# A new order of the 32 experts in a mixture-of-experts stage: small and large ones by turns

## The chip, the core and the metric

The kernel runs on one core of one Trainium2 chip. The metric is the device time of the core in microseconds (us). The kernel before takes 4002.02 us, the median of three runs (3997.02 to 4007.37). The core's engines are named as in the profile: PE (matmuls; PEld its weight loads), DVE (vector work), ACT (activations and copies), POOL (here gathers and scatters through indirect DMA), SP (issues the DMAs of the weights).

## What is computed

The reference is two transformer-like blocks. The change touches the last stage of the second, a mixture of 32 experts over 512 tokens with four experts for each token. Cut to what matters:

```python
logits = (h @ w_router).astype(jnp.float32) + b_router.astype(jnp.float32)
top_val, top_idx = lax.top_k(logits, TOP_K)          # TOP_K = 4 of 32 experts
gates = jax.nn.softmax(top_val, axis=-1)
# for every expert e, on its tokens x:
#   u = x @ w1[e] + b1[e]              # 1024 -> 2048, (gate, linear) pairs
#   a = min(silu-like(u_gate), limit) * (clip(u_lin) + 1)
#   y = a @ w2[e] + b2[e]              # 1024 -> 1024
# the output of a token is the sum of its four y, weighted by gates
```

The last lines are a summary in words of the block function of the reference.

## The kernel before, in words

Before the stage the kernel sorts the experts by the number of tokens that they got (`in_order`). A **rank** is a place in that sorted list; rank 0 is always expert 0, whose first weights are loaded early. `CAPS` fixes how many rows are computed for each rank: 128 for rank 0, 192 for ranks 1 and 2, 128 for ranks 3 to 9, 96 for ranks 10 to 15 and 64 for ranks 16 to 31. "Small" means 64 rows below, "large" 96 and more. Tokens beyond the capacity go to a loop behind the stage, which runs no round in the profiled execution.

The table `ORDER` (L38) lists the ranks in the sequence in which they are computed. In turn i of the loop (L2129) the kernel does `up` of the expert at place i (L1931; `up_half`, L1945, for 192 rows and for the last place), and beside it `down` of the expert at place i-1 (L1964; `down_two`, L1978). An expert draws 12 chunks of weights of 1 MB: eight for `up`, four for `down`. SP loads them into eight buffers (`stage`, L1680). PE multiplies in a fast form that needs a chunk split into two parts: ACT writes the high part `mh` (L1833), DVE the low part `ml` (L1834, 128x2048), three and two buffers of these. `into` (L1872) then issues the matmuls of a chunk for `mh` and `ml` (L1882), and the bias matmuls behind the first chunk (L1886). Experts of 64 rows are "packed": high and low parts of the tokens share one matmul, and on chunks 1 and 4 of `up` and 1 and 2 of `down` the weights are taken unsplit (L1877). So a small expert needs fewer splits and fewer matmuls than a large one.

Beside these a turn holds the preparation of later experts. `Rows` of the next expert transposes its gathered tokens (PE, `pcol`, L1865), and ACT and DVE write them in parts (`ch`, `cl`, L1867 to L1870). `place` of the expert two places on (L2096) calls `gather` (L1897): DVE builds `oh` (L1904), PE computes the token numbers `pi` by four short matmuls (L1907), DVE turns them into an index in a chain of small instructions on `ix` (L1909 to L1914), and POOL fetches the tokens by an indirect DMA (L1916) into `XT`. The results of `up` pass `gated` (L1922, ACT and DVE; packed ones first `whole`, L1888, with an ACT copy and a DVE addition `cl`), those of `down` pass `weighed` (L1956), whose DVE instruction L1959 scales `py` and whose POOL instruction L1961 adds the rows to the output.

Each engine runs its instructions in one fixed order, which a scheduler sets when the program is built; it takes what is ready by its own estimate, so the position of `pi`, of the transposes and of `ml` within a turn depends on which experts are neighbours. The two calls that issue the preparation stand in the loop as

```python
if end and k == (ATC if nparts == 4 else 1) and i < 31:
    xs = [Rows(b[2], "x") for b in got[i + 1][0]]
if end and k == (2 if nparts == 4 else 1) and i < 30:
    got[i + 2] = place(ORDER[i + 2])
```

Of the kernel before, what the change touches and what calls it, by code (L numbers as in the profile page):

```python
# [34 lines left out]

PLAIN = ((1, 4), (1, 2))

ORDER = [0, 16, 17, 18, 1, 19, 20, 21, 2] + list(range(3, 16)) + list(range(22, 32))  # L38

CAPS = [128] + [192] * 2 + [128] * 7 + [96] * 6 + [64] * 16  # L40
OVB = 20
# [87 lines left out]
def tile_two_blocks(ctx: ExitStack, tc: tile.TileContext, I: dict, out: bass.AP, dump=None, stop=None):  # L129
# [1966 lines left out]
    def place(r):  # L2096

        lb = wk.tile([64, 128], F32R, name="lb", tag="lb", bufs=4)
        nc.vector.tensor_copy(lb, (SELP[:, r:r + 1] if r else sel[0:64, 0:1]).to_broadcast([64, 128]))
        pos = lambda t: POS[:, 32 * t + r:32 * t + r + 1]  # L2100
        col = (lambda t: COL[:, t, r, :]) if r else (lambda t: COL0[:, t, 0, :])
        return [gather(pos, col, a, min(128, CAPS[r] - a)) for a in range(0, CAPS[r], 128)], lb
# [23 lines left out]
    xs = [Rows(b[2], "x") for b in got[0][0]]  # L2126
    got[1] = place(ORDER[1])
    before, acts = None, []
    for i in range(33):  # L2129
        steps = [None]  # L2130
        if i < 32:
            blocks, lb = got.pop(i)
            r = ORDER[i]
            e = 0 if r == 0 else nc.sync.value_load(OI[0:1, r:r + 1], min_val=0, max_val=31)
# [18 lines left out]
        for step in steps:  # L2153
# [5 lines left out]
            for k in range(nparts):  # L2159
# [9 lines left out]
                if end and k == (2 if nparts == 4 else 1) and i < 30:  # L2169
                    got[i + 2] = place(ORDER[i + 2])  # L2170
        for _ in todo or ():
# [49 lines left out]
```

## Time and profile before

| | |
|---|---|
| median of three runs | 4002.02 us |
| the profiled execution: time | 3993.1 us |
| the profiled execution: span of the trace | 3991.2 us |
| PE busy | 3767.5 us, 94% of the span |
| DVE busy | 2726.4 us, 68% |
| ACT busy | 1693.6 us, 42% |
| POOL busy | 331.3 us, 8% |
| mean granted clock of PE | 0.961 |
| the expert turns, rank 0 to the end | 2748.6 to 3991 us |

All durations come from one execution, the profiled one. The trace gives each instruction's start and length, the idle time of its engine just ahead of it and what released it. A turn is counted here from the first bias matmul of one `up` (line L1886 with `pu`) to that of the next.

### The profile page before, as it was taken

How to read it: one execution, taken by the hardware profiler on the slowest of the kernel's cores; microseconds unless marked ns; L12 is line 12 of the kernel's file. 1: busy time of each engine (PE TensorE's matmuls, PEld its weight loads, DVE VectorE, ACT ScalarE, POOL GpSimd, SP SyncE). 2: the span in 40 equal slices, each digit the busy share in tenths (PEclk: the TensorE clock that was granted, in tenths of full speed). 3: DMA queues.
4: the chain of work that ended last, by engine and by line, in shares of the span. 5: the costliest groups of instructions: out<-in, count | busy, mean ns of one | idle time of the engine just before them, and what ended most of it. 6: DMA issues, size and time to landing. Idle time of an engine off the chain costs nothing. (4 is left out here: it accounts for less than half of the span.)

```text
span 3991.2 us, 68996 instructions
## 1 busy us (share of the span) xinstructions
PE 3767.5 (94%) x27579; PEld 2829.1 (71%) x27579; DVE 2726.4 (68%) x5439; ACT 1693.6 (42%) x2528; POOL 331.3 (8%) x349
## 2 busy tenths in 40 slices
PE   6998999999999998999999998996999999999997
PEld 4787777888888787776887886674555777664443
DVE  4779875843334778876644535648877899987776
ACT  3234442321212334452222334444655676665555
POOL 0001110000000000110000000001101122223011
PEclk8999999999999998999999997997999999999999
DMA  6122423332422321124544520035979899998996
GB/s 208 45 79 72 120 70 92 125 122 79 127 85 85 103 71 25 38 56 124 169 140 135 123 67 32 1 118 210 373 272 352 314 362 360 370 354 330 375 369 240
DMA packets 353911, 677.75 MB, mean 170 GB/s; under 512 B 118759, under 2 KB 230194, under 8 KB 323474
## 3 DMA queue, kind: packets, MB, share of 16 engines
q1 hardware_dynamic: 343024, 636.89, 45.7%
q0 software_dynamic: 9312, 34.56, 3.4%
q8 instruction: 218, 3.57, 0.4%
q10 hardware_dynamic: 1250, 1.85, 0.1%
q14 instruction: 107, 0.88, 0.1%
HBM read 635.33 MB, written 37.90 MB: 169 GB/s over the span
## 5 line engine op out<-in xcount | busy, mean ns | idle before, releaser
L431 ACT ACTIVATE wh<-wst 128x1024 fp32r<-128x1024 f32 (+2 forms) x222 | 222.8, 1004 | 988.3 <-PE pc L441 520.1
L1834 DVE TENSOR_TENSOR ml<-E,mh 128x2048 fp32r<-128x2048 f32 x236 | 536.1, 2286 | 92.4 <-PE pu L1882 43.9
L1833 ACT ACTIVATE mh<-E 128x2048 fp32r<-128x2048 f32 x236 | 447.8, 1916 | 187.3 <-PE pu L1882 147.0
L441 PE MATMUL px<-Hh,wl 128*128 128x512 f32 (+2 forms) x1216 | 485.9, 400 | 14.5 <-DVE wl L432 14.4
L441 PE MATMUL px<-Hh,wh 128*128 128x512 f32 (+3 forms) x1216 | 486.6, 402 | 13.4 <-ACT wh L431 7.1
L441 PE MATMUL px<-Hl,wh 128*128 128x512 f32 (+3 forms) x1216 | 485.8, 400 | 0.6 <-DVE Hl L419 0.6
L432 DVE TENSOR_TENSOR wl<-wst,wh 128x1024 fp32r<-128x1024 f32 (+2 forms) x222 | 255.7, 1153 | 271.0 <-ACT wh L431 264.1
L1882 PE MATMUL pu<-ml,ch 128*64 128x512 f32 (+2 forms) x968 | 272.7, 399 | 21.1 <-DVE ml L1834 20.5
L1882 PE MATMUL pu<-mh,ch 128*128 128x512 f32 (+1 forms) x968 | 280.5, 405 | 6.9 <-DVE ix L1909 6.1
L441 PEld LDWEIGHTS px<-Hh,wl 128*128 128x128 f32 (+1 forms) x1216 | 231.6, 191 | 74.1 <-DVE wl L432 19.4
L441 PEld LDWEIGHTS px<-Hh,wh 128*128 128x128 f32 (+1 forms) x1216 | 231.9, 191 | 71.7 <-ACT wh L431 9.4
L441 PEld LDWEIGHTS px<-Hl,wh 128*128 128x128 f32 (+1 forms) x1216 | 232.3, 191 | 55.8 <-DVE Hl L419 3.3
L533 DVE SCALAR_TENSOR_TENSOR acc<-ZC,VT,acc 128x272 f32<-128x272 f32 (+2 forms) x600 | 252.0, 482 | 2.7 <-ACT acc L528 2.7
L1882 PEld LDWEIGHTS pu<-mh,ch 128*128 128x128 f32 (+1 forms) x968 | 172.6, 185 | 86.9 <-issue 25.8
L1834 DVE TENSOR_TENSOR ml<-st,mh 128x2048 fp32r<-128x2048 f32 x86 | 196.0, 2286 | 42.5 <-PE pu L1882 24.5
L1882 PEld LDWEIGHTS pu<-ml,ch 128*64 128x64 f32 (+2 forms) x968 | 149.4, 159 | 90.5 <-DVE ml L1834 32.3
L441 PE MATMUL pc<-Hh,wh 128*128 128x256 f32 x672 | 193.2, 288 | 0.9 <-ACT Hh L418 0.9
L441 PE MATMUL pc<-Hl,wh 128*128 128x256 f32 x672 | 191.5, 285 | 0.5 <-DVE Hl L419 0.5
L441 PE MATMUL pc<-Hh,wl 128*128 128x256 f32 (+1 forms) x672 | 190.8, 284 | 0.1
L1833 ACT ACTIVATE mh<-st 128x2048 fp32r<-128x2048 f32 x86 | 163.3, 1918 | 54.3 <-PE pu L1882 31.1
L315 DVE SCALAR_TENSOR_TENSOR as<-adt,CS,as 128x512 f32<-128x512 f32 x224 | 161.5, 750 | 34.5 <-DMA adt<-in_w_ada_dram 19.9
L1138 DVE SCALAR_TENSOR_TENSOR XT<-px,MOD,XT 128x512 f32<-128x512 f32 x66 | 49.5, 750 | 187.5 <-PE px L441 187.1
(602 smaller groups left out, 7872.9 us busy)
## 6 DMA issues: line engine op xcount, KB each, us to landing
E<-in_w_mlp_dram SPq DMA_DIRECT2D x288, 1024.0 KB
st<-in_w_mlp_dram SPq DMA_DIRECT2D x94, 1024.0 KB
wst<-in_w_in_dram SPq DMA_DIRECT2D x29, 1024.0 KB
adt<-in_ada_w_dram SPq DMA_DIRECT2D x96, 256.0 KB
adt<-in_w_ada_dram SPq DMA_DIRECT2D x96, 256.0 KB
wst<-in_ffn_wg_dram SPq DMA_DIRECT2D x22, 1024.0 KB
wst<-in_ffn_wu_dram SPq DMA_DIRECT2D x22, 1024.0 KB
adaw<-in_ada_w_dram SPq DMA_DIRECT2D x16, 1024.0 KB
```

Source lines behind the costliest of these rows:

```text
L315: nc.vector.scalar_tensor_tensor(acc[s], t, c, acc[s], op0=OP.mult, op1=OP.add)
L431: nc.scalar.activation(wh, t[:, :, c0:c0 + n], AF.Copy)
L432: nc.vector.tensor_tensor(wl, t[:, :, c0:c0 + n], f32(wh), op=OP.subtract)
L441: nc.tensor.matmul(p[0:m, 0:n], lhsT=wa[:, k, 0:m], rhs=ha[:, k, a:a + n], start=k == 0 and first, stop=k == nk - 1 and last)
L533: nc.vector.scalar_tensor_tensor(o, z[:, j + a:j + a + n], cw(j), o, op0=OP.mult, op1=OP.add)
L1138: nc.vector.scalar_tensor_tensor(o, src, gate, o, op0=OP.mult, op1=OP.add)
L1833: nc.scalar.activation(wh, t, AF.Copy)
L1834: nc.vector.tensor_tensor(wl, t, f32(wh), op=OP.subtract)
L1882: nc.tensor.matmul(p[0:xa.shape[2]], lhsT=xa[:, kt], rhs=w[part][:, c:c + 512], start=kt == 0 and j == 0, stop=last and j == len(parts) - 1)
```

## The change

Only the table `ORDER` is edited; the rest of the program text is the same.

```diff
-ORDER = [0, 16, 17, 18, 1, 19, 20, 21, 2] + list(range(3, 16)) + list(range(22, 32))
+ORDER = [0, 16, 17, 18, 19, 1, 20, 21, 22, 2, 23, 24, 3, 4, 25, 5, 6, 26, 7, 8, 27, 9, 10, 28, 11, 12, 29, 13, 30, 14, 15, 31]
```

Before, three small experts stand ahead of the first 192-row one and three ahead of the second, then come all large ones (ranks 3 to 15), then the ten small ones left (22 to 31). Now four small ones stand ahead of the first 192-row expert and three ahead of the second, and from then on one small expert alternates with two large ones, at the end with one.

Since the neighbours change, the scheduler places the instructions of every turn anew. First, PE around `pi`. Before, between the turns of ranks 7 and 8 (`py` belongs to `down`, `pu` to the first chunk of the next `up`):

```order
L1882 MATMUL py_30247<-mh,ch 128x512
L1882 MATMUL py_30248<-mh,ch 128x512
L1907 LDWEIGHTS oh
L1907 MATMUL pi<-COL,oh 128x5
...
L1882 MATMUL pu_30380<-mh,ch 128x512
L1882 MATMUL pu_30381<-mh,ch 128x512
```

With the change, in the turn of rank 8, the second large one behind the small rank 26 (`pu` of its own `up`; the first four `ml` belong to the seventh chunk, the next to the eighth and last):

```order
L1882 MATMUL pu_31488<-mh,cl 128x512
L1865 MATMUL pcol<-CF,XT 128x64 x5
L1907 LDWEIGHTS oh
L1907 MATMUL pi<-COL,oh 128x5
...
L1882 MATMUL pu_31485<-ml,ch 128x512
L1882 MATMUL pu_31486<-ml,ch 128x512
L1882 MATMUL pu_31487<-ml,ch 128x512
L1882 MATMUL pu_31488<-ml,ch 128x512
L1882 MATMUL pu_31485<-ml,ch 128x512
```

The four `pi` have moved from the end of a turn to the last two chunks of the up half. Second, DVE at the same places. Before:

```order
L1834 TENSOR_TENSOR ml<-E_25847,mh 128x2048 x2
L1870 TENSOR_TENSOR cl<-pcol,ch 128x512 x2
L1909 COPY ix<-pi 128x5
L1959 SCALAR_TENSOR_TENSOR XT<-py_30247,ix,M_26298 128x512
L1911 TENSOR_SCALAR ix<-ix 128x1
L1913 TENSOR_TENSOR ix<-ix 128x1
L1959 SCALAR_TENSOR_TENSOR XT<-py_30248,ix,M_26298 128x512
L1912 CAST idx<-ix 128x1
L1914 TENSOR_TENSOR ix<-ix 128x1
L1834 TENSOR_TENSOR ml<-E_25847,mh 128x2048
```

With the change, rank 8:

```order
L1834 TENSOR_TENSOR ml<-st_26302,mh 128x2048
L1909 COPY ix<-pi 128x5
L1904 TENSOR_SCALAR oh<-CE,POS 128x64
L1911 TENSOR_SCALAR ix<-ix 128x1
L1913 TENSOR_TENSOR ix<-ix 128x1
L1904 TENSOR_SCALAR oh<-CE,POS 128x64
L1912 CAST idx<-ix 128x1
L1914 TENSOR_TENSOR ix<-ix 128x1
L1904 TENSOR_SCALAR oh<-CE,POS 128x64
L1834 TENSOR_TENSOR ml<-st_26303,mh 128x2048
```

The chain on `ix` now stands between the `ml` of the seventh and of the eighth chunk of `up`. Third, DVE in a small turn. Before, rank 22, the first small one behind the large ones:

```order
L1834 TENSOR_TENSOR ml<-E_25846,mh 128x2048
L1909 COPY ix<-pi 64x5
L1904 TENSOR_SCALAR oh<-CE,POS 128x64
L1911 TENSOR_SCALAR ix<-ix 64x1
L1913 TENSOR_TENSOR ix<-ix 64x1
L1904 TENSOR_SCALAR oh<-CE,POS 128x64
L1912 CAST idx<-ix 64x1
L1914 TENSOR_TENSOR ix<-ix 64x1
L1904 TENSOR_SCALAR oh<-CE,POS 128x64 x2
L1834 TENSOR_TENSOR ml<-E_25846,mh 128x2048
L1834 TENSOR_TENSOR ml<-E_25847,mh 128x2048 x2
L1894 TENSOR_TENSOR cl<-pu_32722,cl 64x512
```

With the change, rank 27, the small one of a triplet:

```order
L1834 TENSOR_TENSOR ml<-E_25846,mh 128x2048
L1909 COPY ix<-pi 96x5
L1904 TENSOR_SCALAR oh<-CE,POS 128x96
L1911 TENSOR_SCALAR ix<-ix 96x1
L1913 TENSOR_TENSOR ix<-ix 96x1
L1904 TENSOR_SCALAR oh<-CE,POS 128x96
L1912 CAST idx<-ix 96x1
L1914 TENSOR_TENSOR ix<-ix 96x1
L1904 TENSOR_SCALAR oh<-CE,POS 128x96 x2
L1834 TENSOR_TENSOR ml<-E_25846,mh 128x2048
L1870 TENSOR_TENSOR cl<-pcol,ch 128x512
L1834 TENSOR_TENSOR ml<-E_25847,mh 128x2048 x2
```

The two read alike but for the `cl` of the transposes behind the second `ml`.

## Rows read from the trace of the kernel before

**Rows 1.** The page, part 1: busy us, share of the span and instructions by engine.
```profile
PE 3767.5 (94%) x27579; PEld 2829.1 (71%) x27579; DVE 2726.4 (68%) x5439; ACT 1693.6 (42%) x2528; POOL 331.3 (8%) x349
```

**Rows 2.** Windows: start and end, length, busy us of PE, PEld, DVE, ACT, POOL; clock, DMA, GB/s.
```profile
3155.50:3488.70 333.20, 332.98 (x1535) 253.94 (x1534) 309.80 (x321) 233.53 (x182) 68.70 (x19) 1.00 0.97 364
3488.70:3603.40 114.70, 111.48 (x511) 75.36 (x510) 102.65 (x114) 74.54 (x61) 27.90 (x8) 1.00 0.94 349
3603.40:3644.90 41.50, 36.47 (x146) 20.16 (x145) 30.86 (x38) 23.93 (x23) 13.23 (x3) 0.96 0.88 325
3644.90:3681.50 36.60, 33.97 (x125) 15.87 (x124) 26.62 (x36) 18.35 (x22) 12.90 (x2) 1.00 0.91 338
3681.50:3894.60 213.10, 202.51 (x734) 94.31 (x733) 163.76 (x208) 129.45 (x134) 23.29 (x12) 1.00 0.99 370
...
2985.00:3018.50 33.50, 33.50 (x128) 16.21 (x127) 26.53 (x34) 21.39 (x23) 6.88 (x4) 1.00 0.95 343
```

**Rows 3.** Waits of the DMA queue SP, 3603 to 3930 us: total, times, longest.
```profile
SPq L1685 <- PE pu L1877: 112.5, 18, 8.3
```

**Rows 4.** Timeline of PE in rank 27, a turn of the tail: start, length.
```profile
3794.11 0.29 PE L1907 MATMUL pi<-COL,oh 128*64 128x5 bf16 x4
3794.33 1.14 PE L1882 MATMUL pu<-ml,ch 128*64 128x512 f32 x4
3795.30 1.09 PE L1882 MATMUL pu<-mh,ch 128*128 128x512 f32 x4
3797.65 1.13 PE L1882 MATMUL pu<-ml,ch 128*64 128x512 f32 x4 [1.26 <-DVE ml L1834]
...
3806.84 1.15 PE L1882 MATMUL pu<-ml,ch 128*64 128x512 f32 x4 [0.59 <-DVE ml L1834]
```

**Rows 5.** Timeline of all engines in rank 24, a turn of the tail.
```profile
3687.30 0.29 PE L1907 MATMUL pi<-COL,oh 128*64 128x5 bf16 x4
...
3687.62 0.16 DVE L1909 COPY ix<-pi 64x5 f32<-64x5 f32 x1 [1.38 <-PE pi L1907]
...
3688.51 2.28 DVE L1834 TENSOR_TENSOR ml<-st,mh 128x2048 fp32r<-128x2048 f32 x1
3689.10 2.49 POOL L1916 DMA_INDIRECT XT<-HD,idx  x1 [5.57 <-PE pu L1882]
3690.71 0.24 DVE L1904 TENSOR_SCALAR oh<-CE,POS 128x64 bf16<-128x64 f32 x1
...
3690.84 1.15 PE L1882 MATMUL pu<-ml,ch 128*64 128x512 f32 x4 [1.26 <-DVE ml L1834]
```

**Rows 6.** Timeline of all engines at the end of rank 9, a large turn.
```profile
3374.32 0.31 PE L1907 MATMUL pi<-COL,oh 128*96 128x5 bf16 x4
...
3374.66 0.16 DVE L1909 COPY ix<-pi 96x5 f32<-96x5 f32 x1
```

**Rows 7.** Timeline in rank 22, the first small turn behind the large ones.
```profile
3618.80 6.68 DVE L1834 TENSOR_TENSOR ml<-E,mh 128x2048 fp32r<-128x2048 f32 x3
3619.23 7.06 POOL L1916 DMA_INDIRECT XT<-HD,idx  x1 [9.98 <-PE pu L1882]
...
3621.14 1.15 PE L1882 MATMUL pu<-ml,ch 128*64 128x512 f32 x4 [1.42 <-DVE ml L1834]
...
3623.34 1.14 PE L1882 MATMUL pu<-ml,ch 128*64 128x512 f32 x4 [1.05 <-DVE ml L1834]
...
3632.85 0.70 PE L1865 MATMUL pcol<-CF,XT 64*128 64x64 f32 x8 [2.56 <-DMA XT<-HD,idx]
...
3634.03 0.62 PE L1882 MATMUL py<-mh,ch 128*96 128x512 f32 x2
3634.49 1.00 PE L1882 MATMUL py<-mh,cl 128*96 128x512 f32 x2
```

**Rows 8.** Timeline in rank 15, the last large turn.
```profile
3589.01 0.69 DVE L1870 TENSOR_TENSOR ch<-pcol,ch 128x512 fp32r<-128x512 f32 x1
...
3589.15 0.71 PE L1882 MATMUL py<-ml,ch 128*96 128x512 f32 x2 [0.74 <-DVE ml L1834]
```

## The prediction

> **What bounds the kernel now.** The page first [rows 1]: TensorE (PE) is busy for 94% of the span, DVE for 68. The windows view, cut at expert turns [rows 2], gives the price of a turn by kind (a turn runs from the bias matmul of one expert's `up` to that of the next). Nine turns of 128 or 96 rows (ranks 4 to 12) take 333.2 us, 37.0 each, with PE busy for all but 0.2 us. Three later ones (ranks 13 to 15) take 38.2 each. Of the turns of 64 rows one without a gap (rank 20) takes 33.5 us; ranks 22 and 23, the first two behind the large ones, take 41.5 and 36.6, and the six of ranks 24 to 29 take 213.1, 35.5 each. In these the DMA share is 0.99, so a reader might take the weights for the bound. The waits of the DMA queue [rows 3] say who waits for whom: SP, which issues the weight transfers, is held most of all by PE's matmuls on unsplit chunks, that is, by buffers that aren't free yet. Transfers wait for consumers, not consumers for transfers. So PE's work is the floor, and what can be won or lost are PE's gaps.
>
> Counted against the turns without a gap, the stage now loses 8.0 + 3.1 us in ranks 22 and 23, 213.1 - 6 x 33.5 = 12.1 us in ranks 24 to 29, and 114.7 - 3 x 37.0 = 3.7 us in ranks 13 to 15: **27 us in all**. The work on PE is the same in any order of the experts, so the change is worth these 27 us less whatever the new order loses.
>
> **Where a gap comes from.** In a tail turn [rows 4] PE stands twice for DVE's `ml`, 1.26 and 0.59 us. DVE's side [rows 5] shows why: PE's four `pi` matmuls of the next gather stand in the middle of the up chunks (at 3687.30), and DVE's instructions on `ix` stand in its queue between two `ml`. DVE can't begin the next `ml` before `pi` is there; it has `pi` at 3687.62, spends 0.9 us on `ix` and `oh`, then 2.28 us on the `ml`, and PE starts again at 3690.84, 3.5 us after `pi` began. Whatever matmuls PE has in its order between `pi` and that `ml` is the cover; what lacks to 3.5 us is a gap. In the large turns without a gap [rows 6] the same `pi` stands at the very end of the turn, with DVE's `ix` behind the turn's last splits; the row of `ix` shows no idle time ahead of it, and PE has no gap. In rank 22 [rows 7] the `ix` stand ahead of three `ml` in a row: gaps of 1.42 and 1.05 us; the gather on POOL takes 7.06 us where it took 2.49 with an `oh` between the `ml` [rows 5], its tokens land late, and the transposes wait 2.56 us for them. After that pause pairs of matmuls take 1.00 us where they took 0.62, which is TensorE's lower clock (1.2 instead of 2.4 GHz) for a few of them; the window's granted clock is 0.96 [rows 2]. The whole is 8.0 us.
>
> **The change, part by part.** One table is edited. It adds no arithmetic, no bytes and no transfer: 32 experts, the same capacities, as many gathers and scatters on POOL, in the same alternation, one register load on SP for each expert. These cost nothing new. The last turn (rank 31) stays last; its `down` neighbour becomes rank 15 instead of 30, which only carries work from one turn to the next. What changes is the fixed order inside the turns, because the scheduler places `pi`, the transposes and the splits anew. Rows of the order show it: for large turns within triplets (one small, two large) `pi` no longer stands at the end but in the up half, and DVE's `ix` between two `ml`. So the kernel gets the tail's pattern in nearly every mixed turn. The prices:
>
> - *Second large turn of a triplet (ranks 6, 8, 10, 12).* Between `pi` and the `ml` that PE needs next stand four matmuls. In the tail there were eight and the gap was 1.26 us [rows 4]; four matmuls are 0.95 us, so the gap is 2.2 us. The tail loses 2.0 us a turn [rows 2] where its gaps sum to 1.85 [rows 4], so 0.1 us is added for each restart: 2.3.
> - *First large turn (ranks 5, 7, 9, 11).* `pi` stands 12 matmuls and more ahead of the next `ml`, as in rank 15, where PE waited 0.74 us for it [rows 8]: 0.8.
> - *Small turn (ranks 25 to 28).* The order is that of rank 22 with one difference: the `cl` or `ch` of the transposes (0.69 us [rows 8]) stands between the first and the second `ml` behind the `ix`. So the gaps are 1.42 and 1.05 [rows 7], plus the 0.7 by which the second and third `ml` are later, plus a gap in the down half as the second in the tail, 0.59 [rows 4], and 0.4 for restarts: 4.2. Since DVE leaves the three `ml` apart there, I let POOL's gather pass as with one `ml` ahead of it, 2.49 us, and charge no wait for its tokens. That is the choice on which most hangs: with the wait it is rank 22's 8.0.
> - Four triplets: 4 x (4.2 + 0.8 + 2.3) = 29.2.
> - *Rank 29* as a small turn of a triplet, 4.2. *Rank 30*, whose order has three `ml` in a row behind the `ix` without anything between, as rank 22: 8.0. *Ranks 13 and 14* beside them 0.8 each.
> - *Ahead of the first 192-row expert* ranks 18 and 19 now stand behind one another. Rank 18 gets the tail's pattern, 2.0; rank 19 the two gaps of rank 22, 2.6. The two 192-row turns keep their length and lose nothing; ranks 20 to 23 stand beside them without a gap, as rank 20 does now [rows 2]. Rank 24, with the tail's second gap alone (0.59 [rows 4]) and a late split, loses 1.0.
>
> Sum of what the new order loses: 29.2 + 4.2 + 8.0 + 1.6 + 2.0 + 2.6 + 1.0 = 49 us; less the 27: **+22 us** on the profiled execution (3993.1 us), 4015. The median of the runs (4002.0) is 8.9 us above that execution, so about 4024.
>
> Bounds. Below: no gap at all is left, -27 us. Above: seven small turns (ranks 19 and 25 to 30) as rank 22, 7 x 8.0 = 56, rank 18 2.0, large turns 4 x 3.1 + 1.6, rank 24 1.0: 73 - 27 = +46, or 4048. The chosen value stands nearer to the upper end since the order of DVE and PE, which is fixed before the run, is rank 22's but for the `cl`.
>
> [...]
>
> **The rivals.**
> (a) *Faster: mixing covers the gaps.* A small expert's eight chunks feed less PE work than a large one's, while both draw 12 chunks of weights; DMA share is 0.99 in the tail and 0.97 among large turns [rows 2]. If splits run further ahead of PE when a longer turn follows a short one, DVE finishes its `ml` before PE asks. The point from which it decides is the 3.5 us from above: a gap goes where PE has that much ready work behind `pi`, in its order or because it was late itself. For it: rank 20, a small turn beside large work, runs without a gap now. Against it: `pi` is PE's own instruction, so DVE can't be ahead of it, however early its data are. All gaps gone is 27 us less, 3975; with a quarter of the new ones left, 12 us, it is 3987.
> The Trainium skill, "Perfetto Trace Analysis" (Optimization Strategy), advises to interleave regimes whose most contended engine differs, which speaks for this case; here SP's waits [rows 3] say that the tail isn't held by transfers, so I give it no more than the rows do.
> (b) *Slower still: rank 22 in every small turn.* The gather passes no `ml`, tokens are late, and the clock drops for some matmuls in each. The upper bound: 4048.
> (c) *No difference.* Small turns cost the tail's 2.0 (8 x 2.0 = 16), second large turns 2.3 (9.2), and all others nothing: 25 against the 27 saved, 4000.
> (d) That the table doesn't do what it says can't be: the order of instructions shows the experts in the new sequence.
>
> **How the numbers follow.** About 0.3% (12 us) is what a measurement of this kernel can tell from no change. My forecast, +22, has 0.44; (b) 0.18; (c) 0.21; (a) 0.17. So faster 0.17, same 0.21, slower 0.62. The range from 3985 to 4048 takes in (b) and (c) whole and that part of (a) in which some gaps stay; left out is most of (a), and worse than (b).
>
> **What would show it.** In the changed profile: first, the second large turns (rank 8, say) are 39 us long with a PE gap of about 2.2 us put down to DVE's `ml`, right behind `pi`; the first large turns about 37.8. Second, small turns of triplets 37.6 us, with gaps of 1.4 and 1.7 us behind `pi`. Third, ranks 22 and 23 have lost their gaps. Fourth, POOL's gathers in small turns take 2 to 3 us and the transposes don't wait for `XT`; if they take 7, it is (b). Wrong would be: `pi` in the up half and yet no gap (a), or PE gaps that end with a weight transfer, which would mean that the buffers no longer cover and the whole reading by order falls.

## The result, and the profile after

The changed kernel takes 4020.5 us (median of nine runs), the kernel before 3996.6 in the same comparison: the ratio is 1.0066, with a 95% interval from 1.0051 to 1.0082. That is slower by more than the 0.3% that such a measurement can tell. The forecast was 4024 us. The profiled execution has a span of 4018.7 us, 27.5 us more than before's 3991.2.

The page, part 1, of the changed kernel answers to [rows 1]. PE has 10.6 us more busy time for the same 27,579 matmuls; the rest of the 27.5 us are gaps.

```profile
span 4018.7 us, 68990 instructions
PE 3778.1 (94%) x27579; PEld 2831.4 (70%) x27579; DVE 2726.6 (68%) x5439; ACT 1687.1 (42%) x2528; POOL 335.1 (8%) x349
```

From the first turn to the end the stage takes 1242.6 us before (2748.6 to 3991.2) and 1273.9 after (2744.8 to 4018.7): **31.3 us more** (it began 3.8 us earlier in this execution). The windows view shows where, in the columns of [rows 2]: ranks 24, 3 and 4 ahead of the first triplet, one triplet (26, 7, 8), the next small turn (27), and rank 30.

```profile
3186.70:3293.90 107.20, 107.20 (x447) 70.18 (x446) 92.61 (x106) 71.23 (x63) 16.02 (x7) 1.00 0.97 369
3410.20:3452.10 41.90, 37.94 (x146) 23.54 (x145) 32.81 (x38) 24.23 (x23) 5.33 (x3) 0.92 0.89 330
3452.10:3488.80 36.70, 36.66 (x147) 24.18 (x146) 29.17 (x36) 19.84 (x19) 4.92 (x2) 1.00 0.94 340
3488.80:3529.90 41.10, 38.87 (x174) 30.00 (x173) 34.87 (x37) 28.21 (x24) 7.97 (x2) 0.96 0.91 345
3529.90:3571.50 41.60, 37.85 (x146) 23.57 (x145) 32.78 (x38) 24.15 (x23) 5.48 (x3) 0.92 0.93 331
3844.70:3883.30 38.60, 35.38 (x145) 20.04 (x144) 33.02 (x36) 27.08 (x24) 4.97 (x3) 1.00 1.00 369
```

The first of these windows is three turns (ranks 24, 3 and 4) without any gap of PE: length and busy time are equal. Ranks 22 and 23 have lost their gaps as well. The triplet is where the time goes. Its first large turn (36.70) is free, but the small turns take 41.9 and 41.6 us and the second large one 41.1, where 33.5 and 37.0 are the turns without a gap [rows 2]. In them the granted clock is 0.92 and 0.96, not 1.00.

The timeline of PE in rank 8, the second large turn, shows both halves of this loss (start, length, then the idle time ahead and what ended it).

```profile
3495.31 1.07 PE L1882 MATMUL pu<-ml,ch 128*128 128x512 f32 x4
3496.22 1.07 PE L1882 MATMUL pu<-mh,ch 128*128 128x512 f32 x4
...
3507.30 0.25 PE L1907 MATMUL pi<-COL,oh 128*128 128x5 bf16 x4
3507.41 1.17 PE L1882 MATMUL pu<-ml,ch 128*128 128x512 f32 x4
3510.81 1.55 PE L1882 MATMUL pu<-ml,ch 128*128 128x512 f32 x4 [2.23 <-DVE ml L1834]
3512.16 1.91 PE L1882 MATMUL pu<-mh,cl 128*128 128x512 f32 x4
3513.87 1.55 PE L1882 MATMUL pu<-mh,ch 128*128 128x512 f32 x4
3515.26 0.63 PE L1882 MATMUL py<-mh,ch 128*128 128x512 f32 x2
```

Behind `pi` stand four matmuls, then PE waits 2.23 us for DVE's `ml`; the prediction said 2.2. But the twelve matmuls after the gap then need 4.45 us (3510.81 to 3515.26), where three groups of four normally start 0.91 us apart, 2.73 us in all. The granted clock of this stretch is 0.62: for most of it PE ran at the lower of its two levels (1.2 instead of 2.4 GHz), which costs another 1.7 us.

All engines in rank 27, a small turn, answer to [rows 5, 7]:

```profile
3543.87 0.30 PE L1907 MATMUL pi<-COL,oh 128*96 128x5 bf16 x4
...
3544.21 0.16 DVE L1909 COPY ix<-pi 96x5 f32<-96x5 f32 x1 [1.47 <-PE pi L1907]
...
3545.32 2.28 DVE L1834 TENSOR_TENSOR ml<-E,mh 128x2048 fp32r<-128x2048 f32 x1
3545.76 2.68 POOL L1916 DMA_INDIRECT XT<-HD,idx  x1 [14.18 <-PE pu L1882]
3547.52 0.68 DVE L1870 TENSOR_TENSOR cl<-pcol,ch 128x512 fp32r<-128x512 f32 x1
...
3547.66 1.14 PE L1882 MATMUL pu<-ml,ch 128*64 128x512 f32 x4 [1.59 <-DVE ml L1834]
3548.12 4.48 DVE L1834 TENSOR_TENSOR ml<-E,mh 128x2048 fp32r<-128x2048 f32 x2
...
3550.46 1.97 PE L1882 MATMUL pu<-ml,ch 128*64 128x512 f32 x4 [1.66 <-DVE ml L1834]
```

DVE itself waits 1.47 us for `pi`, then does `ix` and `oh`, then the `ml` that PE needs. Two gaps follow, 1.59 and 1.66 us, and after the second the next matmuls are slow here too (four take 1.97 us, where the four after the first gap take 1.14). POOL's gather takes 2.68 us with the `cl` of L1870 between the `ml`, as forecast.

The waits of the DMA queue SP from 3410 to 3921 us (total, times, longest) answer to [rows 3]: SP still waits for the consumers of its buffers.

```profile
SPq L1685 <- DVE ml L1834: 283.8, 102, 6.0
SPq L1685 <- PE pu L1877: 60.1, 10, 6.8
```

The waits of PE from 3293 us (rank 25) to 3921 are two rows in all. Every one of the 34.1 us of gaps ends with DVE's `ml`, none with a weight transfer or with late tokens.

```profile
PE pu L1882 <- DVE ml L1834: 25.5, 15, 2.4
PE py L1882 <- DVE ml L1834: 8.6, 12, 1.1
```

### The profile page after: what moved, and what is told of

Its sections match the earlier page's. It is cut to its first block, busy times and chain, and to the rows that moved or that the text cites. A ratio compares the mean times of both kernels' runs of the same rounds, so it can differ in the third digit from the quotient of the medians.

```text
span 4018.7 us, 68990 instructions
## 1 busy us (share of the span) xinstructions
PE 3778.1 (94%) x27579; PEld 2831.4 (70%) x27579; DVE 2726.6 (68%) x5439; ACT 1687.1 (42%) x2528; POOL 335.1 (8%) x349
## 5 line engine op out<-in xcount | busy, mean ns | idle before, releaser
L1834 DVE TENSOR_TENSOR ml<-E,mh 128x2048 fp32r<-128x2048 f32 x233 | 528.7, 2285 | 95.5 <-issue 38.5
L1882 PEld LDWEIGHTS pu<-ml,ch 128*64 128x64 f32 (+2 forms) x968 | 149.7, 160 | 98.1 <-DVE ml L1834 41.7
L315 DVE SCALAR_TENSOR_TENSOR as<-adt,CS,as 128x512 f32<-128x512 f32 x224 | 161.4, 748 | 37.8 <-DMA adt<-in_w_ada_dram 20.3
```

The source lines that it names most:

```text
L315: nc.vector.scalar_tensor_tensor(acc[s], t, c, acc[s], op0=OP.mult, op1=OP.add)
L1834: nc.vector.tensor_tensor(wl, t, f32(wh), op=OP.subtract)
L1882: nc.tensor.matmul(p[0:xa.shape[2]], lhsT=xa[:, kt], rhs=w[part][:, c:c + 512], start=kt == 0 and j == 0, stop=last and j == len(parts) - 1)
```

## The experiments

The theory: DVE's queue is in order, so an instruction that waits for `pi` holds the next `ml`; the gap is 3.5 us less the PE work that stands behind `pi`; and a long gap brings the lower clock. The rivals: weights that land late, late tokens, the head part of the table (four small experts ahead of the first 192-row one), or the mixing as such. In what follows "S" is the small turn of a triplet, "L1" and "L2" its first and second large one. In the changed kernel the triplets of ranks 26, 27 and 28 have S 41.9, 41.6, 39.6; L1 36.7, 37.4, 37.6; L2 41.1 each. The triplet ahead of them (25, 5, 6) has S 38.7, L1 36.6, L2 40.9.

### The two parts of the table, each alone

**e3_head_only**: the head part without the mixing.

```diff
-ORDER = [0, 16, 17, 18, 1, 19, 20, 21, 2] + list(range(3, 16)) + list(range(22, 32))
+ORDER = [0, 16, 17, 18, 19, 1, 20, 21, 22, 2] + list(range(3, 16)) + list(range(23, 32))
```

> One part of the change alone: four small experts ahead of the first 192-row one and three ahead of the second (ranks 19 and 22 moved forward), then all large ones and the small ones left, as before. Theory: ranks 18 and 19 lose 1.6 and 3 to 4 us, rank 22 saves its 8 us there, but rank 23 takes its place as the first small turn behind the large ones and loses about 8 instead of 3: 0 to +5 us against the kernel before. Rival (the four ahead of the first 192-row expert cost the time, by weights that come late there): +10 us or more.

Measured: 4000.5 us, ratio 1.0006 [0.9993, 1.0019]: no difference. The windows of this run show that rank 22, now beside large work, takes 33.6 us without a gap, and that rank 23, which has taken its place behind the large turns, takes over its 41.7 us.

```profile
3067.90:3101.50 33.60, 33.60 (x130) 16.70 (x129) 27.74 (x41) 21.50 (x24) 5.05 (x2) 1.00 1.03 389
3652.90:3694.60 41.70, 36.36 (x146) 20.28 (x145) 30.77 (x37) 23.85 (x23) 13.14 (x3) 0.96 0.88 325
```

The 8 us belong to the place in the sequence, not to the expert [rows 2].

**e4_mix_only**: the mixing with the head as before.

```diff
-ORDER = [0, 16, 17, 18, 1, 19, 20, 21, 2] + list(range(3, 16)) + list(range(22, 32))
+ORDER = [0, 16, 17, 18, 1, 19, 20, 21, 2, 22, 23, 3, 4, 24, 5, 6, 25, 7, 8, 26, 9, 10, 27, 11, 12, 28, 13, 29, 14, 30, 15, 31]
```

> The other part alone: the head as before, then from rank 22 on one small expert to two large ones, at the end one to one. Theory: PE gaps of 2.2 us in each second large turn and of 1.5 and 1.7 us in each small one, as in the changed kernel, +18 to +30 us against the kernel before. Rival (the head is what costs): 0 to +8 us.

Measured: 4024.2 us, ratio 1.0065 [1.0052, 1.0078]. The three triplets that answer to those above (their small experts are here ranks 25, 26 and 27) have S 40.9, 41.5, 39.6 and L2 41.1 each. The whole loss is the mixing; the head part costs and gives nothing. Two other turns differ from the changed kernel's. Rank 29 takes 44.3 us: its gather takes 7.06 us and the transposes wait 4.04 us for the tokens. And rank 6, the first L2, takes 39.3 us, though its gap behind `pi` is as long as the others':

```profile
3360.73 1.20 PE L1882 MATMUL pu<-ml,ch 128*128 128x512 f32 x4 [2.24 <-DVE ml L1834]
3361.76 1.07 PE L1882 MATMUL pu<-mh,cl 128*128 128x512 f32 x4
```

Here the matmuls after the gap run at their normal length. So a gap of 2.2 us brings the lower clock often, but not always.

### Moving the wait for `pi`

**e5_place_first**: from turn 10 of the loop on, that of rank 23, the preparation of the expert two places on is issued ahead of the transposes of the next, not behind them. `pi` then stands a few matmuls earlier, with more PE work behind it.

```diff
+                if end and k == (2 if nparts == 4 else 1) and 10 <= i < 30:
+                    got[i + 2] = place(ORDER[i + 2])
                 if end and k == (ATC if nparts == 4 else 1) and i < 31:
                     xs = [Rows(b[2], "x") for b in got[i + 1][0]]
-                if end and k == (2 if nparts == 4 else 1) and i < 30:
+                if end and k == (2 if nparts == 4 else 1) and i < 10:
                     got[i + 2] = place(ORDER[i + 2])
```

> The new order; from the turn of rank 23 on, the whole gather of the expert two places on is issued ahead of the transposes of the next expert instead of behind them. Up to rank 2 nothing changes. In the fixed order pi moves ahead as in the first experiment, and the ix behind it on DVE. Theory: the mixed turns come out as there: small ones 38.5 instead of 41.7 us, second large ones 38 instead of 41, no lower clock behind the smaller gaps, -20 to -25 us against the changed kernel, 3994 to 4002 us. What is left in the small turns (about 2 us) is not pi but ACT, which stands for PE's transposes ahead of the last split. Rival (the first experiment's mixed turns were shorter because its early turns had been delayed and weights had gathered): 4012 us or more.

Measured: 4003.8 us, ratio 1.0021 [1.0009, 1.0033], just above what was expected, and two thirds of the loss gone. S takes 39.4, 38.4, 38.3, L2 37.9, 38.2, 38.0. The windows of rank 8 and rank 27 in this run:

```profile
3496.91:3534.78 37.87, 37.13 (x173) 28.78 (x172) 34.78 (x37) 27.97 (x24) 7.93 (x2) 1.00 0.97 365
3534.78:3573.21 38.43, 35.09 (x145) 21.78 (x144) 32.64 (x38) 23.72 (x22) 3.70 (x3) 1.00 0.99 364
```

L2's gap behind `pi` fell from 2.23 to 0.74 us, and with it 1.74 us of busy time (38.87 to 37.13) for the same work, at a clock of 1.00: the clock's share of a gap, measured by its absence. In S the busy time fell by 2.76 us (37.85 to 35.09). What is left in S is another wait, shown by the timeline of all engines:

```profile
3549.16 0.60 ACT L1867 ACTIVATE ch<-pcol 128x512 fp32r<-128x512 f32 x1 [1.86 <-PE pcol L1865]
3549.66 3.70 ACT L1833 ACTIVATE mh<-E 128x2048 fp32r<-128x2048 f32 x2
...
3551.59 4.49 DVE L1834 TENSOR_TENSOR ml<-E,mh 128x2048 fp32r<-128x2048 f32 x2 [0.96 <-ACT mh L1833]
...
3553.94 1.13 PE L1882 MATMUL pu<-ml,ch 128*64 128x512 f32 x4 [2.05 <-DVE ml L1834]
```

ACT, in order as well, waits 1.86 us for the transposes, its next `mh` is late by that, DVE waits for `mh`, and PE for `ml`. So in S the gaps hardly shrank (rank 27: 3.75 us in the changed kernel, 3.33 here); what went there are the slow matmuls.

**e1_pi_ahead_after** and **e2_pi_ahead_before**: `oh` and `pi` are issued two parts of the loop earlier; the chain on `ix` and the transfer stay in their part, but ahead of the transposes of the next expert, not behind them. The edit was made in the changed kernel (e1) and in the one before (e2). In these two the experts beside the 192-row ones compute on other rows, since a gather there lands before the rows that it replaces are read.

```diff
+                if end and k == (0 if nparts == 4 else 0) and i < 30:
+                    later = place(ORDER[i + 2], True)
+                if end and k == (2 if nparts == 4 else 1) and i < 30:
+                    got[i + 2] = [g() for g in later[0]], later[1]
                 if end and k == (ATC if nparts == 4 else 1) and i < 31:
                     xs = [Rows(b[2], "x") for b in got[i + 1][0]]
-                if end and k == (2 if nparts == 4 else 1) and i < 30:
-                    got[i + 2] = place(ORDER[i + 2])
```

> The new order of experts, but the gather of the expert two places on is issued in two pieces: oh and the pi matmuls ahead of the first part of down, the ix chain and the POOL transfer where the whole stood. The scheduler then puts pi further ahead of the ml that follows ix: in the small turns of triplets two to four packed chunks ahead of the eighth, in the first large turns at the end of the turn before, in the second ones 12 matmuls and 8 transposes ahead instead of 4 matmuls. Theory (the loss is DVE's wait for pi between two ml, plus TensorE's lower clock behind it): the gaps of 1.5, 1.9 and 2.2 us behind pi go, small turns of triplets come to about 36 us, second large ones to 37, and the program to 3965 to 3985 us, 35 to 55 below the changed kernel. Rival (weights: mixing makes transfers the bound, pi only stands near): the turns keep their length, gaps move to other ml or to transfers, 4010 to 4025 us. Rival (the order of ml and cl in DVE's queue, not pi): 4005 to 4020 us.

> The old order with the gather issued in the same two pieces. Theory: the 27 us that ranks 13 to 15, 22 and 23 and the tail lose by the same wait go for the most part, 3970 to 3982 us, a version faster than both kernels and within 10 us of the new order with the same edit, since PE's work is the same in either. Rival (weights): the tail's DMA share is 0.99, so its turns stay at 35.5 us and the program within 5 us of the kernel before.

Measured: 4040.4 us, ratio 1.0112 [1.0097, 1.0127], and 4020.9, ratio 1.0061 [1.0048, 1.0074]. Both totals missed. The triplets of e1 became shorter, as the theory has it, but not by as much as expected (S 38.2 to 38.7 us for an expected 36, L2 37.9 to 38.2 for 37): they are about as long as in e5. And the turns of the head became longer, because the transposes there now wait for tokens. The row of PE's timeline is from rank 19's turn in e1, which takes 47.7 us instead of 37.3:

```profile
2916.85 1.94 PE L1865 MATMUL pcol<-CF,XT 128*128 128x128 f32 x8 [8.90 <-DMA XT<-HD,idx]
```

In e2 the head (ranks 0 to 2) lost 35 us in the same way, while the tail's turns fell only from 35.5 to 35.1. So an earlier `pi` does help where it has cover; this edit paid more elsewhere, which is why e5 leaves the head as it was.

**e8_place_later**: for the experts behind place 11 the whole preparation is issued one turn later, in the middle of `up`, where much work stands behind `pi`.

```diff
+                if kt == 5 and 11 < i + 1 < 32:
+                    got[i + 1] = place(ORDER[i + 1])
...
-                if end and k == (2 if nparts == 4 else 1) and i < 30:
+                if end and k == (2 if nparts == 4 else 1) and i + 2 <= 11:
```

> The new order; from rank 3 on the gather of an expert is issued one turn later, at the sixth chunk of up in the turn right ahead of its own, so its tokens come later and the transposes move back: in second large turns behind all matmuls but the last chunk, with the last split ahead of them on ACT; in first large turns the transposes partly as before. The small turns keep the transposes ahead of the last split. Theory: second large turns 37 to 38 us instead of 41, small ones 39 instead of 41.7, 3995 to 4006 us. Rival (with a whole turn less between gather and use, tokens land too late: transposes wait for XT): PE gaps put down to the transfer of XT, 4015 us or more.

Measured: 4103.9 us, ratio 1.0275 [1.026, 1.029]. It missed; its rival was right. PE's timeline in rank 8 shows that the gather lands too late:

```profile
3531.78 1.09 PE L1865 MATMUL pcol<-CF,XT 64*128 64x64 f32 x8 [6.67 <-DMA XT<-HD,idx]
```

### Changing the cover, not `pi`

**e6_last_chunk**: experts of more than 64 rows take the parts of their last chunk in the usual sequence, so that `ml` comes last, not first. `pi` and DVE's wait stay.

```diff
-            parts = self.parts if not last else self.parts[::-1]
+            parts = self.parts[::-1] if last and self.packed else self.parts
```

> The new order; the last chunk of up and of down of large experts is multiplied with mh first and ml last, as all other chunks, instead of ml first. The need for that ml moves 8 matmuls (1.9 us) back. In the second large turns the order of pi, ix and ml stays, so theory (the gap is 3.5 us less the matmuls between pi and the ml that is needed) says that their gap of 2.2 us shrinks to 0.3 to 0.5 and the lower clock behind it goes: 41.0 to about 37.4 us in ranks 6, 8, 10, 12; first large turns, where pi moves to the down half, lose nothing; small ones keep 3 to 4 us of gaps. Together -12 to -20 us, 4000 to 4008. Rival (the ml is late by itself, by ACT or the weights): the gap moves behind the 8 matmuls with its length, 4015 to 4022.

Measured: 4019.2 us, ratio 1.0059 [1.0045, 1.0073]; the total missed. PE in rank 8 in this run:

```profile
3514.60 1.19 PE L1882 MATMUL pu<-ml,ch 128*128 128x512 f32 x4 [0.39 <-DVE ml L1834]
...
3517.56 0.73 PE L1882 MATMUL py<-ml,ch 128*128 128x512 f32 x2 [0.85 <-DVE ml L1834]
```

The gap behind `pi` fell from 2.23 to 0.39 us with eight more matmuls between `pi` and the `ml` that is needed, and the matmuls behind it keep their normal length (1.19 us); but a gap of 0.85 us stands in the down half, and L2 takes 39.1, 38.9, 38.6, not the expected 37.4. The scheduler also placed the small turns anew, and in ranks 27 to 29 the `cl` left its place between two `ml`. The timeline of rank 27 in this run shows what that does:

```profile
3546.97 6.68 DVE L1834 TENSOR_TENSOR ml<-E,mh 128x2048 fp32r<-128x2048 f32 x3
3547.44 7.05 POOL L1916 DMA_INDIRECT XT<-HD,idx  x1 [9.96 <-PE pu L1882]
...
3562.15 0.55 PE L1865 MATMUL pcol<-CF,XT 96*128 96x96 f32 x4 [2.20 <-DMA XT<-HD,idx]
```

This is rank 22 of the kernel before [rows 7], rival (b) of the prediction, in three small turns: in ranks 27, 28 and 29 the gather takes 7.05 to 7.07 us (2.68 in rank 27 of the changed kernel), the transposes wait 2.2 to 3.7 us for tokens, and the turns take 41.9, 43.7 and 43.7 us. In ranks 25 and 26 no tokens are late (37.1 and 40.0 us).

**e7_last_chunk_before**: the same edit in the kernel before.

```diff
-            parts = self.parts if not last else self.parts[::-1]
+            parts = self.parts[::-1] if last and self.packed else self.parts
```

> The old order with the same edit of the last chunk. The scheduler also places the tail anew: pi in the first third of a turn, the transposes at its end. Theory: large turns stay at 37.0, ranks 13 to 15 lose their 1.1 us, and in the tail the chain on ix stands between the splits of the third and fourth chunk with 8 matmuls of cover, about 1.6 us of gap, less behind it: 3985 to 4000 us. Rival (the tail is bound by weights at a DMA share of 0.99): tail turns stay at 35.5 whatever pi does.

Measured: 3996.1 us, ratio 1.0000 [0.9987, 1.0013]. The total lies in the expected range, but for neither of the reasons given: ranks 13 to 15 stay at 38.3 to 38.5 us, and the tail's turns, which were to be placed anew, keep their 35.3 to 35.6 us and their gaps. In the large turns `pi` stands at the end, so there was no gap behind it to cover.

### Taking the waiting instructions off DVE

**e9_ix_off_dve**: the copy of `pi` goes to ACT and the small `ix` instructions to POOL, so that no `ix` stands in DVE's queue.

```diff
-        nc.vector.tensor_copy(ix[:, 0:5], pi[:, 0:5])
+        nc.scalar.activation(ix[:, 0:5], pi[:, 0:5], AF.Copy)
...
-        nc.vector.tensor_copy(idx, ix[:, 5:6])
+        nc.gpsimd.tensor_copy(idx, ix[:, 5:6])
```

> The new order; pi is copied from PSUM by ACT, and the four small instructions on ix that follow run on POOL, ahead of the gather that they feed. PE's order in the triplets stays that of the changed kernel, pi included; what goes is DVE's wait for pi between two ml. In second large turns the copy stands on ACT behind the last split, in small ones ahead of it. Theory (DVE's wait is the loss): the gap of 2.2 us in second large turns goes, 41.0 to 37 us; in small turns the two gaps of 1.5 and 1.7 become one of about 2 us, since now ACT waits for pi ahead of the last split (0.2 + 1.9 + 2.3 us behind pi, 12 matmuls of cover): 41.5 to 38.5. Together -20 to -30 us, 3990 to 4002. Rival (the gaps come from the order on PE, from splits that are late anyway, or from the weights): PE's order is the same, so they stay: 4015 to 4025. Against the theory's number: POOL's small instructions may wait for DVE, so tokens could come late; then the transposes wait for XT.

Measured: 4040.1 us, ratio 1.0108 [1.0087, 1.013]. It missed. DVE's timeline in rank 6 names the reason:

```profile
3397.32 0.74 DVE L1904 TENSOR_SCALAR oh<-CE,POS 128x64 bf16<-128x64 f32 x4 [2.84 <-PE pi L1907]
3397.98 2.29 DVE L1834 TENSOR_TENSOR ml<-E,mh 128x2048 fp32r<-128x2048 f32 x1
```

The wait for `pi` is still there. `oh` has two buffers, and that of the gather after can't be written before PE's `pi` has read the older one; without `ix` to wait for, the scheduler put `oh` in the same place. `ix` was one waiter of two. That the run is also some 20 us slower than the changed kernel comes mostly from the small turns, as the expectation had feared: the index now comes from POOL, and in ranks 25 to 28 the transposes wait 1.3 to 5.1 us for tokens.

**e12_oh_off_dve**: as e9, with `oh` on POOL as well.

```diff
-                nc.vector.tensor_scalar(oh[:, t], slot[:, 0:m], pos(t), None, op0=OP.is_equal)
+                nc.gpsimd.tensor_scalar(oh[:, t], slot[:, 0:m], pos(t), None, op0=OP.is_equal)
...
-        nc.vector.tensor_copy(ix[:, 0:5], pi[:, 0:5])
+        nc.scalar.activation(ix[:, 0:5], pi[:, 0:5], AF.Copy)
```

> As the kernel with ix on ACT and POOL, and the four oh of each gather run on POOL too. In that kernel the oh took the place of ix: only two buffers hold oh, so the oh of the next gather waits for the pi that reads the older one, between the same two ml. Now nothing on DVE waits for pi; PE's order in the triplets is still that of the changed kernel. Theory, mended (whatever on DVE depends on pi holds back the ml behind it): in second large turns the gap of 2.0 to 2.2 us is gone, 36.9 us instead of 40.7; in small turns the first of the two gaps (1.5) goes, the one for ACT's late last split (about 2 us) stays. If POOL, which now has nine instructions for a gather, is in time: 3985 to 4000 us in all; if it is late, the transposes wait for XT by 1 to 6 us in each small turn: 4005 to 4040. Rival (these ml are late by themselves): the gap in second large turns stays at 2 us.

Measured: 4042.9 us, ratio 1.0116 [1.0095, 1.0138], just above what was expected with a late POOL. Two opposite things make it up. PE in rank 8 of this run:

```profile
3533.57 0.26 PE L1907 MATMUL pi<-COL,oh 128*128 128x5 bf16 x4
3533.68 2.09 PE L1882 MATMUL pu<-ml,ch 128*128 128x512 f32 x8
3535.61 1.07 PE L1882 MATMUL pu<-mh,cl 128*128 128x512 f32 x4
```

PE's order is that of the changed kernel, four short `pi`, four `ml` and again four `ml`, but with nothing on DVE that waits for `pi` the second group follows at once. The 2.23 us are gone, the slow matmuls too (1.07), and L2 takes 37.6 us. So in L2 DVE's wait for `pi` is the cause, and neither PE's order, the weights nor the mixing as such is enough. In S one gap ahead of `ml` is left of three (1.91 us in rank 27, where the changed kernel has 3.75 in all), the one that stands for ACT's late `mh`. But POOL pays for it:

```profile
3567.20 2.58 POOL L1904 TENSOR_SCALAR oh<-CE,POS 128x96 bf16<-128x96 f32 x4 [12.69 <-PE pi L1907]
3569.78 4.24 POOL L1911 TENSOR_SCALAR ix<-ix 96x1 f32<-96x1 f32 x1
```

An `ix` instruction on 96 numbers takes 4.24 us on POOL beside DVE's `ml` (the next one 0.19); the index comes late, the transposes wait for tokens, and S takes 42.2 to 44.8 us.

### Both edits together

**e10_both_in_new_order** and **e11_both_in_old_order** take e5's earlier `place` and e9's move of `ix` together, in the new order of experts and in the old one (there from turn 21 on, the small turns alone).

```diff
-        nc.vector.tensor_copy(ix[:, 0:5], pi[:, 0:5])
+        nc.scalar.activation(ix[:, 0:5], pi[:, 0:5], AF.Copy)
...
+                if end and k == (2 if nparts == 4 else 1) and 21 <= i < 30:
+                    got[i + 2] = place(ORDER[i + 2])
```

> The new order with both edits: the gather issued ahead of the transposes from the turn of rank 23 on, and ix on ACT and POOL. Theory: pi is early and DVE doesn't wait for it; left are ACT's waits for the transposes ahead of the last split in small turns (about 2 us) and 0.7 us in some large ones: 3985 to 3998 us, at or below the kernel before. Rival: as the kernel with the early gather alone, 4000 to 4008.

> The old order with both edits, the early gather from rank 15's turn on. Meant as a version that beats both kernels: ranks 13 to 15 lose 1 us less each, rank 22 finds its tokens in time (41.4 to 36 us), the tail keeps one gap of about 1 us by the two buffers for ml (35.5 to 34.6): 3978 to 3990 us. Rival (the tail is bound by weights at a DMA share of 0.99): 3993 us or more.

Measured: e10 4005.4 us, ratio 1.0027 [1.0012, 1.0043], as its rival had it: L1 rose to 39.0 and 39.1 us in two triplets of three. **e11 takes 3988.2 us, ratio 0.9982 [0.997, 0.9995]**, in the expected range. Its interval lies below 1, but the gain of 0.18% is less than the 0.3% that such a measurement can tell, so it is not shown that e11 beats the kernel before. Its windows for rank 22 and for ranks 24 to 29 answer to [rows 2]:

```profile
3607.80:3644.40 36.60, 34.76 (x149) 19.61 (x148) 30.19 (x33) 24.10 (x25) 14.40 (x12) 1.00 0.92 346
3679.70:3890.80 211.10, 204.72 (x738) 95.04 (x737) 161.49 (x178) 129.37 (x140) 27.10 (x36) 1.00 0.98 374
```

Rank 22 fell from 41.5 to 36.6 us, the six tail turns from 213.1 to 211.1 (35.2 each, where 34.6 were expected): part of the 27 us that the change was after, had without a new order. Ranks 13 to 15, which were to lose 1 us each, stay at 37.8 to 38.3.

## Why the prediction was right, and which term was off

**The direction and the total.** +22 us were forecast, +24 measured between the medians, and +31.3 in the stage of the profiled executions. The steps, one by one:

- *PE's work is the floor, gaps are what counts.* Right: where there is no gap, the turns keep their length (ranks 24, 3 and 4 take 107.2 us together, for 33.5 + 2 x 37.0 = 107.5).
- *The 27 us of before go.* Right: ranks 22 and 23 have no gap any more, and e3 shows that rank 22's 8 us stay with the place. But 8.0 is too much for rank 22. A turn also holds `down` of the expert before it; rank 22 stands behind a large one and has 146 matmuls, rank 20, whose 33.5 us served as the measure, 128 [rows 2]. Small turns behind a large one, with a clock of 1.00, have PE busy for 35.4 us (ranks 28 and 30 of the changed kernel), and the large turn that follows gets some of it back (36.4 to 36.7 instead of 37.0, with 147 matmuls). So rank 22 loses about 6 us, 5.0 of them gaps [rows 7]. The same shift is in every S and L1 of the new order, where it nearly cancels within a triplet.
- *A gap is 3.5 us less the cover.* Right for L2: 2.23 to 2.37 against 2.2; e5 and e6 changed the cover and the gap followed; e12 took the waiter away, and it went. In S the first gap is 1.47 to 1.59 us against 1.42 in all four, but the second only in ranks 26 to 28 near the 1.75 (1.86, 1.66, 1.54; rank 25 has 0.29), and the gap in the down half is 0.50 to 0.86 against 0.59. Two of the four L1 have no gap, two 1.08 and 1.10, against 0.8. Over the four triplets the gaps sum to 25.8 us, where the prediction's gap terms make 27.0 (4 x (3.76 + 0.8 + 2.2)). What the prediction did not see is that `oh` is a second waiter, so that taking `ix` off DVE is no cure (e9).
- *The gather passes POOL in 2.49 us because of the `cl`.* Right in its length: 2.58 to 2.69 in ranks 26 to 29. In e6 the `cl` had gone from there in ranks 27 to 29, and the gather took 7.05 us and more. But the `cl` is not what it takes: rank 30 has none, and its gather took 2.35 us. The prediction charged rank 30 like rank 22, though ranks 28 and 29 of the kernel before had already shown a short gather under three `ml` in a row (rows at the end). The Trainium skill, "SBUF — State Buffer" ("Who interferes with whom"), says that a DVE instruction with two SBUF inputs contends with a GpSimd instruction that reads SBUF, but also that `tensor_tensor`, the operation of `ml`, did not stall a DMA in a probe of its own. Here the gather of rank 27 in e6 ends 0.8 us after the third `ml`, so on the second point this measurement says otherwise.
- *Restarts at 0.1 us each.* **This is the term that failed.** It was read from the tail, where gaps are 1.26 and 0.59 us and no clock is lost. Behind L2's 2.2 us the lower clock costs 1.5 to 1.7 us (busy time of the four L2 against e5). In S, where 0.4 were charged, it costs about 2.8 in ranks 26 and 27 (clock 0.92), and nothing in ranks 25 and 28 (clock 1.00). Over the four triplets that is about 12 us where the terms for restarts make 2.0. The prediction had the warning in its own rows, since rank 22's window has a clock of 0.96 [rows 2], but charged it to the late tokens alone.

In the triplet of rank 27 the 120.0 us (41.56 + 37.44 + 41.05) are 107.5 without gaps (33.5 + 2 x 37.0), 7.1 of gaps, 4.5 of clock; about 1 us is not accounted for. The four triplets lost 44.3 us instead of 29.2 (25.8 of gaps, about 12 of clock, about 6 not accounted for), and rank 29 7.2 instead of 4.2. That the total still came out near is luck in other terms: rank 30 lost 5.1, not 8.0; ranks 13 and 14 together 2.2 less than charged; the last turn, which was not forecast, takes 61.2 instead of 64.3 us. With rank 19 (1.2 more) and small differences elsewhere this makes 31 where 22 stood.

**The rivals.** (a), that mixing covers the gaps, fell: in the mixed turns PE waits 2.7 to 4.2 us in S and 2.2 to 2.4 in L2, and what ends the waits is DVE's `ml`, not a transfer. The Trainium skill, "Perfetto Trace Analysis" (Optimization Strategy), says that interleaving regimes may help where the most contended engine changes over time. Here no run bears that out: even e5, with L2's gaps mostly gone, stays 0.21% above before; and PE is the busiest engine both among the large turns (332.98 of 333.20 us) and in the tail (202.51 of 213.10) [rows 2]. (b), rank 22 in every small turn, did not happen in the changed kernel, where no transposes of a triplet wait for tokens, but did in three small turns of e6. (c), 4000 us, fell: the small turns of the triplets wait 2.7 to 4.2 us, and two of them have slow matmuls as well, where 2.0 were charged.

## What to carry to other kernels

A table that only renames the order of equal work still decides what stands next to what in every in-order queue. Look for the short preparing instruction that waits for another engine (here `ix` and `oh`, 0.2 us each) and count the work that its producer has behind it: what lacks is a gap, and it recurs in each turn. Price a gap of 2 us with the slow matmuls that may follow it, not only by its length, and before moving a waiter to another engine ask which instruction the scheduler will put in its place.

## What the runs showed of the hardware

- **The clock behind a gap.** After 2.23 us of idle time PE's next twelve matmuls took 4.45 us instead of 2.73. The gap's length alone does not tell: after 2.24 us in rank 6 of e4 the next four took 1.20 us and after 2.05 us in e5's small turn 1.13, the normal lengths of those forms, while in rank 6 of e9 four took 1.56 us after a gap of 2.00 (1.19 is normal there). In the changed kernel two gaps of 1.59 and 1.54 us left rank 28 at a clock of 1.00, two of 1.59 and 1.66 rank 27 at 0.92. What decides was not settled.
- **POOL beside DVE's `ml`.** A gather took 7.05 us under three `ml` in a row (e6, and 7.06 in rank 22 before [rows 7]), 2.68 with a `cl` between. But in rank 30 of the changed kernel, also under three `ml` in a row, it took 2.35 us. The long one ends 0.8 us after the third `ml`, the short one 0.8 us after the first. Under three `ml` in a row the traces part by the start: those that began 0.42 to 0.47 us into the first `ml` took 7.05 to 7.07 us, those that began 0.73 to 0.80 us into it 2.32 to 2.36, ranks 28 and 29 of the kernel before among them. Under two in a row the start does not part them (rank 8 of e12 began 0.20 us in and took 3.03, rank 25 of the changed kernel 1.24 and took 4.11), so the reason stays open. The rows of rank 30, then of rank 28 before:

```profile
3859.45 6.69 DVE L1834 TENSOR_TENSOR ml<-E,mh 128x2048 fp32r<-128x2048 f32 x3
...
3860.21 2.35 POOL L1916 DMA_INDIRECT XT<-HD,idx  x1 [12.92 <-PE pu L1882]
```

```profile
3830.63 2.29 DVE L1834 TENSOR_TENSOR ml<-st,mh 128x2048 fp32r<-128x2048 f32 x1
...
3831.36 2.36 POOL L1916 DMA_INDIRECT XT<-HD,idx  x1 [5.42 <-PE pu L1882]
3832.84 4.49 DVE L1834 TENSOR_TENSOR ml<-E,mh 128x2048 fp32r<-128x2048 f32 x2
```

- **Two in-order queues, not one.** With DVE's wait moved, ACT's wait for the transposes (1.86 us) leaves a gap of 2.05 us in the same turn. A version with ACT's wait gone as well was not tried, nor one with a third buffer for `ml` or `oh`.
